# Remainders of all float32r splits on VectorE: one layer of a hybrid streaming encoder on one core

## Chip, cores and metric

The kernel runs on one core of one Trainium2 chip. The metric is the device time of one launch in microseconds, the median of several runs. The profiles are of one execution each, taken by the hardware profiler.

## The reference

One layer works on x, 1024 tokens by 1024 channels in float32, with a conditioning vector c. Both sub-layers are normed before and after, shifted, scaled and gated by rows of `c_act @ w_ada`:

```python
mod = c_act @ w_ada[l] + b_ada[l]
h = _rms(x, g_pre_mix[l]) * (1.0 + sc_m) + sh_m
p = h @ w_in[l] + b_in[l]                     # 1024 x 3072
cv = _conv_mixer(...)                         # GLU, causal depthwise conv(31), group norm, swish
hg = _hgrn2(...)                              # 4 heads, gated linear recurrence over 128 states
y = jnp.concatenate([cv, hg], axis=-1) @ w_out[l]
x = x + gt_m * _rms(y, g_post_mix[l])
h = _rms(x, g_pre_ffn[l]) * (1.0 + sc_f) + sh_f
y = jnp.square(jax.nn.relu(h @ w_up[l])) @ w_down[l]   # 4096 hidden
x = x + gt_f * _rms(y, g_post_ffn[l])
```

## The kernel before

Every large product is made from three matmuls in float32r. Each operand is split into a high part, which is the operand rounded to float32r, and a low part, the remainder: high x high, high x low and low x high are summed in PSUM. So each weight block of 128 x 1024 and each activation block is split once. ScalarE copies it into float32r (the high part), and another engine subtracts that copy from the original (the low part). This subtraction is what the change is about. Its two inputs and its output lie in SBUF.

Three places split. `split` (line 347) serves the weights of the input projection (class `Loads`, line 569), the output weights (`load_wo`, line 1140), the conv and head outputs (`conv_out`, line 774, and `put_mix`, line 639) and the summed gate rows (line 1074). `halve` (line 1312) serves channel mixing: its weights and sums come through the class `Feed` (line 1373), its activations through `hc_split` (line 1330). The first three weight blocks are split in small pieces by `first_w` (line 524), and the first activations by `h_evac` (line 504); these two have engines of their own choice, which the change leaves.

The order of the work on every engine is fixed when the program is built. The class `Weave` (line 209) keeps a planned clock for each engine. One main stream issues the large matmuls; side streams (loads, splits, evacuations, norms, heads) are Python generators that yield the time or the condition at which they go on, and `poll` runs whichever is due. The costs of the plan stand in lines 293 to 296:

```python
V = wv.engine(nc.vector, "V", lambda op, n: 0.16 + n / 930)
A = wv.engine(nc.scalar, "A", lambda op, n: 0.22 + n / 1190)
G = wv.engine(nc.gpsimd, "G", lambda op, n: 0.55 + n / (1350 if op == "tensor_scalar" else 520))
S = wv.engine(nc.sync, "S", lambda op, n: n * 1.455 / 1024)
```

On the chip each engine takes its instructions in that order, and semaphores hold them until their inputs are there and their buffers are free. `split` and `halve` choose GpSimd (G) where its planned end is at most 0.5 us (`LO_G`, line 62) behind VectorE's (V). All weight and row loads are issued on SyncE's queue (S); a load waits there until the buffer that it writes has been read by the split before.

The stages, in the order of time: the input norm and the first three blocks of the input projection; the other blocks (`ptG`, `ptU`, `ptV` by tokens, `pj` by channels), beside which the conv group (`cv`) and the four HGRN heads run; the output projection (`pout`) with the norm, gate and residual of each token tile (`out_tile`, line 1203); the second norm, transposed by TensorE (`pt` in `h2_half`, line 1230); then the up projection (`pup`) and the down projection (`al` and `be`), which use a seven-product scheme on 2 x 2 blocks, so that VectorE also forms sums of blocks.

Two chains matter below. In a head (`head_att`, line 838) seven levels follow each other, h = 1 to 64: TensorE makes a group of small matmuls `pl`, VectorE multiplies halves of Q and K in place by a decay, and the next level reads them; for the levels 1 to 8 VectorE also writes the result through a mask (four COPY_PREDICATED). Between the levels TensorE is given `pj` or `pout` matmuls. In the output projection a tile's chain is: VectorE adds the two parts of the product (`pout`), ScalarE sums squares, GpSimd makes the reciprocal root (`pr`), VectorE scales and adds the residual, ScalarE sums squares again, GpSimd makes the second root (`rx`) and scales the tile; four such tiles are needed by the first transposes `pt`.

Of the kernel before, what the change touches and what calls it, by code (L numbers as in the profile page):

```python
# [7 lines left out]
F32 = mybir.dt.float32  # L8
# [4 lines left out]
ALU = mybir.AluOpType  # L13
# [45 lines left out]


CSTEP = 8
NEAR, EXTRA, LO_G, DLAT, DLAT0 = 1.0, 0.4, 0.5, 2.0, 2.0
XIDLE, HIDLE, WIDLE = 0.3, 0.3, 0.3
XRANK, MRANK, RMODS, RCONV, RLOAD, RNORM = 0, 1, 7, 6, 3.5, 1.5
MODS_AT = 1
# [104 lines left out]
def free_size(ap):  # L170
    n = 1
    for d in ap.shape[1:]:
        n *= d
    return n
# [34 lines left out]
class Weave:  # L209
# [30 lines left out]
    def after(self, key, extra=None):  # L240
        return max(self.t[key], self.now) + (EXTRA if extra is None else extra)
# [47 lines left out]
def block_kernel(ctx: ExitStack, tc: tile.TileContext, x, vecs, masks, rows, vrow, crow, wada_t, wada_n,  # L289
                 win0, win, wint, toep, cbias, wout, wup, wdn, out):  # L290
    nc = tc.nc
    wv = Weave()
# [3 lines that stand above are left out]
# [3 lines left out]
    after, idle = wv.after, wv.idle  # L299
# [47 lines left out]
    def split(src, hi, lo):  # L347

        A.activation(hi, src, AF.Copy)
        yield after("A", 0)  # L350
        n = free_size(src)
        if max(wv.t["G"], wv.now) + 0.55 + n / 520 <= max(wv.t["V"], wv.now) + 0.16 + n / 930 + LO_G:
            G.tensor_tensor(lo, src, hi.bitcast(F32), ALU.subtract)
            yield after("G", 0)
        else:
            V.tensor_tensor(lo, src, hi.bitcast(F32), ALU.subtract)
            yield after("V", 0)


    vec = const.tile([P, V_N], F32, name="vec")  # L360
# [208 lines left out]
    class Loads:  # L569
# [6 lines left out]
        def stream(self):  # L576
            for src in self.srcs:
                yield stage.room()
                st = stage.next()
                S.dma_start(st.f, src)  # L580
                yield wv.t["S"] + DLAT
                yield self.ring.room(2)
                hi, lo = self.ring.next().r, self.ring.next().r
                yield from split(st.f, hi, lo)
                stage.give(st)
                self.ready.append((hi, lo, wv.now))
# [52 lines left out]
    def put_mix(kt, half, fn):  # L639


        if (kt // 2, half) not in mix:
            mix[kt // 2, half] = pair()
        hi, lo = mix[kt // 2, half]
        sl = HALF[kt % 2]
        full = half512("mfull")
        fn(full)
        yield from split(full, hi.r[:, sl], lo.r[:, sl])
        for n in range(4):
            marks.t["mix", kt, half * 4 + n] = wv.now  # L650
# [123 lines left out]
    def conv_out(s):  # L774

        y = ys[s]
        yield after("V")
        yield room(2)
        sz, z = new(), new()
        for h in range(2):  # L780
            yield aux_free
            pb = ps1("cpb")
            for b in range(4):
                TE.transpose(pb[:, b * P:(b + 1) * P], y.f[:, (4 * h + b) * P:(4 * h + b + 1) * P], ident)
            yield after("PE", 0.2)
            pv = pb.rearrange("p (b c i) -> p c b i", c=4, i=CB)
            zv = z.f[:, HALF[h]].rearrange("p (c b i) -> p c b i", c=4, i=CB)
            for c in range(4):
                A.activation(zv[:, c], pv[:, c], AF.Identity, bias=col(V_GNB + c), scale=col(V_GNG + c))
            done1(pb, "A")  # L790
        y.release()
        A.activation(sz.f, z.f, AF.Sigmoid)
        yield after("A")
        V.tensor_tensor(z.f, z.f, sz.f, ALU.mult)
        sz.release()
        yield after("V", 0)
        yield room(2)
        hi, lo = mix[s % 2, s // 2] = pair()
        yield from split(z.f, hi.r, lo.r)
        z.release()  # L800
        for n in 2 * s, 2 * s + 1:
            for k in range(4):
                marks.t["mix", k, n] = wv.now
# [508 lines left out]
    def halve(src, hi, lo, keep=False):  # L1312

        A.activation(hi.r, src.f, AF.Copy)
        yield after("A", 0)
        key, eng = ("G", G) if max(wv.t["G"], wv.now) + 2.5 <= max(wv.t["V"], wv.now) + 1.2 + LO_G else ("V", V)
        eng.tensor_tensor(lo.r, src.f, hi.r.bitcast(F32), ALU.subtract)
        if not keep:
            src.release()
        yield after(key, 0)  # L1320

    def plus(out, a, b, op=ALU.add):
        V.tensor_tensor(out.f, a.f, b.f, op)
# [6 lines left out]
    def hc_split(name, src, keep):  # L1330

        hi, lo = pair()
        hc.setdefault(name, []).append((hi, lo))
        yield from halve(src, hi, lo, keep)
        marks.t["hc", name, len([1 for m in marks.t if m[:2] == ("hc", name)])] = wv.now
# [73 lines left out]
    def up_single(self, names, raws, more):  # L1409
        yield from halve(raws[0], *more)  # L1410
        self.put(names[0], *more)
# [5 lines left out]
    def up_2a(self, names, raws, more):  # L1417
        g = names[0][1]
        a21, a22, a11 = raws
        yield plus(a22, a21, a22)  # L1420
        t = store(s1u, g, a22)
        yield plus(a21, a11, a21)
        wv.add(up_s3(self, names[1], a21, more[2:]), RLOAD)
        yield plus(a11, a22, a11)
        store(s2u, g, a11)
        yield from halve(a11, *more[:2], True)
        self.put(names[0], *more[:2])
        yield t
        free((a22, a11))
# [494 lines left out]
```

## Time and profile before

| | us |
|---|---|
| median of 3 runs (1122.4 to 1123.09) | 1122.75 |
| the profiled execution | 1120.97 |
| its span | 1119.2 |
| VectorE busy, 774 instructions | 705.2 |
| ScalarE busy, 651 instructions | 458.5 |
| GpSimd busy, 191 instructions | 279.8 |
| of that 65 splits of 128 x 1024 | 169.0 |
| one split of 128 x 512 on GpSimd | 1.3 |

In the views "busy" is the time in which an engine had an instruction running; the time of an instruction that is held up by another engine counts as busy too. Line numbers in the rows are mostly those of two helpers (L236 for all engines of the plan, L1808 and L1812 for TensorE, L414 for GpSimd's roots), so that groups are told apart by the names of the tiles: `s` is any of the large SBUF buffers.

### The profile page before, as it was taken

What the parts mean: (1) busy time and instruction counts of PE and PEld (TensorE: products, weight loads), DVE (VectorE), ACT (ScalarE), POOL (GpSimd) and SP (SyncE); (2) the same over time, 40 slices, a digit from 0 to 9 for tenths busy, and PEclk for the clock granted to TensorE, in tenths of its full rate; (3) what the DMA queues carried; (4) which work ended last, traced back from release to release, by engine and by line L of the source; (5) the groups of instructions that cost most, each with busy time, mean ns of one, the idle gap of its engine ahead of it and who ended that gap; (6) DMA issues with size and microseconds to landing.
All of it is one profiled execution on the core that took longest, in us unless ns stands there. A gap on an engine that the chain in (4) does not pass through costs nothing.

```text
span 1119.2 us, 18058 instructions
## 1 busy us (share of the span) xinstructions
PE 1084.5 (97%) x7524; PEld 882.9 (79%) x7524; DVE 705.2 (63%) x774; ACT 458.5 (41%) x651; POOL 279.8 (25%) x191
## 2 busy tenths in 40 slices
PE   6999999999998799989999999999999999999997
PEld 2777877878886688868888888888888888888886
DVE  3548476146789841756766965433267979996952
ACT  6732201013355243657442324466643434354530
POOL 5121013003345210672201411134400002303511
PEclk8999999999999999989999999999999999999999
DMA  9523524845212223353679744325577866675711
GB/s 366 204 75 115 160 80 135 223 138 137 75 39 96 78 75 133 125 213 133 226 257 345 287 143 171 113 70 186 196 253 273 313 219 235 217 284 176 290 50 76
DMA packets 57105, 195.27 MB, mean 174 GB/s; under 512 B 6208, under 2 KB 10688, under 8 KB 56768
## 3 DMA queue, kind: packets, MB, share of 16 engines
q1 hardware_dynamic: 57024, 194.13, 50.7%
q8 instruction: 59, 0.97, 0.4%
q14 instruction: 22, 0.18, 0.0%
HBM read 158.39 MB, written 35.72 MB: 173 GB/s over the span
## 4 chain that ended last, share of the span: by engine, by line
PE 83%; DVE 8%; POOL 3%; DMA 3%; issue 2%; ACT 1%; SPq 0%; POOLq 0%; DVEq 0%; ACTq 0%
PE pup L1808 27%; PE al L1808 15%; PE be L1808 12%; DVE s L236 8%; PE pout L1808 6%; PE pj L1808 6%; PE ptG L1808 4%; PE ptV L1808 3%; PE pf L1808 3%; POOL s L236 1%; PE po L1808 1%; PE pt L1812 1%; PE cv L1808 1%; PE pl L1808 1%; PE pm L1808 1%
## 5 line engine op out<-in xcount | busy, mean ns | idle before, releaser
L236 DVE TENSOR_TENSOR s<-s,s 128x1024 fp32r<-128x1024 f32 (+3 forms) x328 | 403.3, 1267 | 91.2 <-ACT s L236 58.2
L236 ACT ACTIVATE s<-s 128x1024 fp32r<-128x1024 f32 (+2 forms) x305 | 294.8, 997 | 343.5 <-DVE s L236 209.6
L236 POOL TENSOR_TENSOR s<-s,s 128x1024 fp32r<-128x1024 f32 (+2 forms) x81 | 187.4, 2320 | 566.3 <-ACT s L236 501.9
L1808 PE MATMUL pup<-s,s 128*128 128x512 f32 x1344 | 308.1, 390 | 0.0
L1808 PEld LDWEIGHTS pup<-s,s 128*128 128x128 f32 x1344 | 251.4, 188 | 51.9
L1808 PE MATMUL al<-s,s 128*128 128x512 f32 x768 | 175.0, 389 | 0.0
L1808 PEld LDWEIGHTS al<-s,s 128*128 128x128 f32 x768 | 144.1, 188 | 30.3 <-DVE s L236 0.4
L1808 PE MATMUL be<-s,s 128*128 128x512 f32 x576 | 131.0, 389 | 0.0
L1808 PEld LDWEIGHTS be<-s,s 128*128 128x128 f32 x576 | 108.1, 188 | 22.5
L1808 PE MATMUL pj<-s,s 128*128 128x512 f32 x432 | 107.3, 400 | 0.0
L1808 PE MATMUL pout<-s,s 128*128 128x512 f32 x384 | 95.1, 403 | 2.0 <-DVE s L236 2.0
L1808 PEld LDWEIGHTS pj<-s,s 128*128 128x128 f32 x432 | 79.8, 190 | 16.1
L1808 PEld LDWEIGHTS pout<-s,s 128*128 128x128 f32 x384 | 72.7, 193 | 17.5 <-DVE s L236 2.7
L236 DVE TENSOR_TENSOR s<-pup,s 128x1024 f32<-128x1024 f32 x24 | 29.3, 1222 | 46.7 <-PE pup L1808 46.5
L236 DVE SCALAR_TENSOR_TENSOR s<-pup,s 128x1024 f32<-128x1024 f32 x16 | 19.6, 1225 | 53.3 <-PE pup L1808 50.3
L236 DVE SCALAR_TENSOR_TENSOR s<-s,c_act,s 128x1024 f32<-128x1024 f32 x28 | 35.9, 1281 | 25.5 <-DMA s<-in_wada_n 25.4
L1808 PE MATMUL ptG<-s,s 128*128 128x512 f32 x192 | 46.2, 395 | 0.0
L1808 PE MATMUL ptU<-s,s 128*128 128x512 f32 x192 | 46.2, 395 | 0.0
L1808 PE MATMUL ptV<-s,s 128*128 128x512 f32 x192 | 46.2, 401 | 0.0
L1808 PEld LDWEIGHTS ptV<-s,s 128*128 128x128 f32 x192 | 37.0, 194 | 8.0
L236 ACT ACTIVATE junk<-s 128x1024 bf16<-128x1024 f32 (+1 forms) x30 | 30.0, 998 | 32.5 <-DVE s L236 25.3
L1808 PEld LDWEIGHTS ptG<-s,s 128*128 128x128 f32 x192 | 35.3, 188 | 7.7 <-ACT s L236 0.3
(124 smaller groups left out, 801.5 us busy)
## 6 DMA issues: line engine op xcount, KB each, us to landing
s<-in_wdn SPq DMA_DIRECT2D x72, 512.0 KB
s<-in_wup SPq DMA_DIRECT2D x56, 512.0 KB
s<-in_wada_n SPq DMA_DIRECT2D x32, 512.0 KB
s<-in_x SPq DMA_DIRECT2D x16, 512.0 KB
s<-in_wada_t SPq DMA_DIRECT2D x16, 512.0 KB
u<-s SPq DMA_DIRECT2D x16, 512.0 KB
s<-u SPq DMA_DIRECT2D x16, 512.0 KB
s<-in_wint SPq DMA_DIRECT2D x12, 512.0 KB
```

Source lines behind the costliest of these rows:

```text
L236: return op(*a, **k)
L1808: return self.te.matmul(out, lhsT=lhsT, rhs=rhs, **k)
L1812: return self.te.transpose(out, in_, identity)
```

## The change

Both choices fall away: `split` and `halve` always subtract on VectorE. The constant `LO_G` goes too.

```diff
-NEAR, EXTRA, LO_G, DLAT, DLAT0 = 1.0, 0.4, 0.5, 2.0, 2.0
+NEAR, EXTRA, DLAT, DLAT0 = 1.0, 0.4, 2.0, 2.0
...
         A.activation(hi, src, AF.Copy)
         yield after("A", 0)
-        n = free_size(src)
-        if max(wv.t["G"], wv.now) + 0.55 + n / 520 <= max(wv.t["V"], wv.now) + 0.16 + n / 930 + LO_G:
-            G.tensor_tensor(lo, src, hi.bitcast(F32), ALU.subtract)
-            yield after("G", 0)
-        else:
-            V.tensor_tensor(lo, src, hi.bitcast(F32), ALU.subtract)
-            yield after("V", 0)
+        V.tensor_tensor(lo, src, hi.bitcast(F32), ALU.subtract)
+        yield after("V", 0)
...
         A.activation(hi.r, src.f, AF.Copy)
         yield after("A", 0)
-        key, eng = ("G", G) if max(wv.t["G"], wv.now) + 2.5 <= max(wv.t["V"], wv.now) + 1.2 + LO_G else ("V", V)
-        eng.tensor_tensor(lo.r, src.f, hi.r.bitcast(F32), ALU.subtract)
+        V.tensor_tensor(lo.r, src.f, hi.r.bitcast(F32), ALU.subtract)
         if not keep:
             src.release()
-        yield after(key, 0)
+        yield after("V", 0)
```

GpSimd loses 66 instructions and VectorE has 66 more; TensorE, ScalarE and SyncE have as many as before. Since the plan's clock of VectorE runs on further, the order of the other instructions changes in places too. Three places follow.

VectorE in the stage of the last two heads, before. `s_3544`, `s_3328` and `s_3327` are Q, K and the decay of head 3, `s_3140`, `s_3039` and `s_3038` those of head 2, `s_3768` is a gate of a head.

```order
L236 COPY_PREDICATED s_682<-msk,pl 32x8x16 x4
L236 TENSOR_TENSOR s_3140<-s_3140,s_3038 128x8x64
L236 TENSOR_TENSOR s_3039<-s_3039,s_3038 128x8x64
L236 TENSOR_TENSOR s_3038<-s_3038 128x8
L236 SCALAR_TENSOR_TENSOR s_3768<-pj_3547,vec,s_3768 128x1024
L236 TENSOR_TENSOR s_3544<-s_3544,s_3327 128x256x2
L236 TENSOR_TENSOR s_3328<-s_3328,s_3327 128x256x2
L236 TENSOR_TENSOR s_3327<-s_3327 128x256
L236 COPY_PREDICATED s_682<-msk,pl 32x8x8x2 x4
L236 TENSOR_TENSOR s_3544<-s_3544,s_3327 128x128x4
```

The same place now. Head 3 has `s_3536`, `s_3322` and `s_3321`, head 2 `s_3134`, `s_3033` and `s_3032`; the gate is `s_3745`.

```order
L236 COPY_PREDICATED s_682<-msk,pl 32x8x16 x4
L236 TENSOR_TENSOR s_3743<-s_3234,s_3742 128x1024
L236 SCALAR_TENSOR_TENSOR s_3745<-pj_3539,vec,s_3745 128x1024
L236 TENSOR_TENSOR s_3134<-s_3134,s_3032 128x8x64
L236 TENSOR_TENSOR s_3033<-s_3033,s_3032 128x8x64
L236 TENSOR_TENSOR s_3032<-s_3032 128x8
L236 TENSOR_TENSOR s_3536<-s_3536,s_3321 128x256x2
L236 TENSOR_TENSOR s_3322<-s_3322,s_3321 128x256x2
L236 TENSOR_TENSOR s_3321<-s_3321 128x256
L236 COPY_PREDICATED s_682<-msk,pl 32x8x8x2 x4
L236 TENSOR_TENSOR s_3748<-s_883,s_3747 128x1024
L236 TENSOR_TENSOR s_3768<-s_3769,s_3767 128x1024
```

Three splits stand in the row that were GpSimd's: of a conv output (`s_3743`) and of two blocks of the output weights (`s_3748`, `s_3768`).

GpSimd in the norm behind the output projection, before. `s_4515` and `s_4531` are the first two token tiles, `rx` and `pr` their roots.

```order
L236 TENSOR_SCALAR s_4515<-s_4515,rx_4643 128x1024
L236 TENSOR_SCALAR pr<-pss 128x1
L414 TENSOR_TENSOR pr<-pr,mhalf 128x1
L236 TENSOR_TENSOR s_4578<-s_4575,s_4577 128x1024
L236 TENSOR_SCALAR rx_4685<-ssx2ss 128x1
L414 TENSOR_TENSOR rx_4685<-rx_4685,mhalf 128x1
L236 TENSOR_SCALAR s_4531<-s_4531,rx_4685 128x1024
```

The same place now.

```order
L236 TENSOR_SCALAR s_4515<-s_4515,rx_4643 128x1024
L236 TENSOR_SCALAR pr<-pss 128x1
L409 TENSOR_TENSOR pr<-pr,mhalf 128x1
L236 TENSOR_SCALAR rx_4685<-ssx2ss 128x1
L409 TENSOR_TENSOR rx_4685<-rx_4685,mhalf 128x1
L236 TENSOR_SCALAR s_4531<-s_4531,rx_4685 128x1024
```

The split of the first up weights (`s_4578`) is gone from between the tiles; it stands in VectorE's row now.

TensorE at the first transposes, before: three blocks of the last token tile's output projection, the transposes `pt` of the first four tiles, and that tile's fourth block. The part shown begins in the third block.

```order
L1808 MATMUL pout<-s_3925,s_3748 128x512 x2
L1808 MATMUL pout<-s_3926,s_3748 128x512 x2
L1808 MATMUL pout<-s_3925,s_3749 128x512 x2
L1812 MATMUL pt_4793<-msk,s_4515 128x128
L1812 MATMUL pt_4793<-msk,s_4531 128x128
L1812 MATMUL pt_4793<-msk,s_4573 128x128
L1812 MATMUL pt_4793<-msk,s_4550 128x128
L1808 MATMUL pout<-s_3979,s_3748 128x512 x2
```

The same place now.

```order
L1802 MATMUL pout<-s_4155,s_4292 128x512 x2
L1802 MATMUL pout<-s_4156,s_4292 128x512 x2
L1802 MATMUL pout<-s_4155,s_4293 128x512 x2
L1806 MATMUL pt_4770<-msk,s_4515 128x128
L1806 MATMUL pt_4770<-msk,s_4531 128x128
L1806 MATMUL pt_4770<-msk,s_4573 128x128
L1806 MATMUL pt_4770<-msk,s_4550 128x128
L1802 MATMUL pout<-s_3747,s_2897 128x512 x2
```

The transposes now follow on the last block of the tile before, and all eight blocks of the last tile (48 matmuls) come behind them, where there were five (30).

## The prediction

> **What bounds the kernel now.** I read the page first, for who is busy and where; then the windows of 40 us, for the stages; then TensorE's waits inside the stages that have gaps.
>
> ```profile
> span 1119.2 us, 18058 instructions
> PE 1084.5 (97%) x7524; PEld 882.9 (79%) x7524; DVE 705.2 (63%) x774; ACT 458.5 (41%) x651; POOL 279.8 (25%) x191
> ```
>
> TensorE (PE) is busy for 97% of the span, so at most 34.7 us are to be had anywhere. The windows say where (columns: busy time and count of PE, PEld, DVE = VectorE, ACT, POOL = GpSimd; granted clock, DMA share, GB/s).
>
> ```profile
> 320.00:360.00 40.00, 37.79 (x638) 29.79 (x637) 36.38 (x52) 23.02 (x41) 18.05 (x8) 1.00 0.24 81
> 360.00:400.00 40.00, 33.00 (x435) 26.94 (x434) 30.21 (x50) 15.00 (x41) 14.44 (x8) 0.96 0.27 82
> 480.00:520.00 40.00, 37.92 (x183) 30.73 (x182) 19.84 (x15) 29.55 (x40) 21.67 (x23) 0.93 0.47 168
> 600.00:640.00 40.00, 40.00 (x178) 33.12 (x177) 38.80 (x28) 11.15 (x12) 16.50 (x7) 1.00 0.83 306
> 920.00:960.00 40.00, 40.00 (x178) 33.14 (x177) 37.79 (x27) 16.00 (x16) 10.24 (x4) 1.00 0.73 248
> 960.00:1000.00 40.00, 40.00 (x179) 33.10 (x178) 38.43 (x30) 19.05 (x19) 7.59 (x3) 1.00 0.72 253
> ```
>
> In the channel-mixing stage (the last three rows) TensorE has no gap: a faster split there buys nothing, and VectorE is almost full, so there the change can only do harm. The gaps that a split can reach lie in 320 to 400 us (the last two HGRN heads beside the end of the input projection) and around 480 us (the norm behind the output projection). TensorE's waits in 330 to 410 us and in 410 to 530 us:
>
> ```profile
> PE pl L1808 <- DVE s L236: 7.6, 5, 4.3
> PE cpb L1812 <- DVE s L236: 0.7, 1, 0.7
> PE pS L1808 <- DVE s L236: 0.7, 1, 0.7
> PE pl L1808 <- ACT s L236: 0.2, 1, 0.2
> PE pt L1812 <- POOL s L236: 2.0, 1, 2.0
> PE pout L1808 <- DVE s L236: 2.0, 1, 2.0
> ```
>
> The first four rows are 9.2 us, nearly all behind VectorE. Why VectorE is late there is seen in its timeline beside GpSimd's:
>
> ```profile
> 355.22 9.02 POOL L236 TENSOR_TENSOR s<-s,s 128x1024 fp32r<-128x1024 f32 x3 [5.15 <-ACT s L236]
> 358.20 3.82 DVE L236 TENSOR_TENSOR s<-s,s 128x512 f32<-128x512 f32 x2
> 361.95 2.83 DVE L236 TENSOR_TENSOR s<-s 128x512 f32<-128x512 f32 x1
> 366.59 1.29 DVE L236 TENSOR_TENSOR s<-s,s 128x512 f32<-128x512 f32 x2
> 149.43 0.69 DVE L236 TENSOR_TENSOR s<-s 128x512 f32<-128x512 f32 x1
> ```
>
> The pair that takes 1.29 us alone takes 3.82 beside a GpSimd split, and the 0.69 us product takes 2.83: each such meeting costs VectorE 2.1 to 2.5 us. Over a long row of nothing but splits it is the same:
>
> ```profile
> 923.22 16.26 DVE L236 TENSOR_TENSOR s<-s,s 128x1024 fp32r<-128x1024 f32 x14
> 941.49 31.14 DVE L236 TENSOR_TENSOR s<-s,s 128x1024 fp32r<-128x1024 f32 x16 [2.01 <-ACT s L236]
> ```
>
> The first row runs undisturbed: 16.26/14 = 1.16 us a split. The second has six GpSimd splits beside it: (31.14 - 16 x 1.16)/6 = 2.1 us lost for each.
>
> **The change, part by part.**
>
> ```profile
> L236 POOL TENSOR_TENSOR s<-s,s 128x1024 fp32r<-128x1024 f32 x65 | 169.0, 2604 | 526.7 <-ACT s L236 501.2 <-issue 13.5 <-DMA s<-in_win 7.1
> ```
>
> *What is moved.* All 65 full splits and one half split go from GpSimd to VectorE: GpSimd loses 169.0 us and a little, VectorE gains 66 x 1.16 = 77 us of work and loses the meetings. A meeting costs 2.1 us and a moved split 1.16, so VectorE comes out ahead wherever it was busy when GpSimd split, and pays 1.16 us where it was idle. I expect its total to stay near 705 us (690 to 725).
>
> *Head stage, 320 to 400 us.* The chain is: a `pl` group on TensorE, VectorE multiplies Q and K in place (1.29 us for both), the next `pl` group; VectorE's masked copies and now the splits lie between, and TensorE's `pj` matmuls are the cover. I walked it level by level with these durations, four masked copies at 1.77 us and 18 `pj` matmuls at 4.1:
>
> ```profile
> 364.80 1.77 DVE L236 COPY_PREDICATED s<-msk,pl 32x128 f32<-32x128 uint32 x4
> 434.56 41.06 PE L1808 MATMUL pout<-s,s 128*128 128x512 f32 x180
> ```
>
> (18 x 41.06/180; the row is of `pout`, the same shape.) For head 2, a level costs VectorE 3.9 to 5.9 us with its one or two splits and TensorE 5.3 us of cover; for head 3, behind the new order, a level is 4.0 to 6.4 us against 3.2 to 7.9. At each `pl` the products of the level before are ready 1 us or more ahead. So the whole of the 9.2 us goes, and with it the slow matmuls behind its longest wait:
>
> ```profile
> 354.69 3.03 PE L1808 MATMUL pj<-s,s 128*128 128x512 f32 x12
> 366.71 1.06 PE L1808 MATMUL pl<-s,s 128*32 128x16 f32 x64 [4.31 <-DVE s L236]
> 367.70 4.03 PE L1808 MATMUL pj<-s,s 128*128 128x512 f32 x12
> 374.85 0.74 PE L1808 MATMUL pl<-s,s 128*32 128x16 f32 x64
> ```
>
> 1.06 - 0.74 + 4.03 - 3.03 = 1.3 us. Together 10.5; what is late next are splits that find their high part or their weights not there, for which I keep 1 us back. Term: -9.5 (bounds -10.5, and 0 if those waits fill the whole place).
>
> *Output projection, 450 to 500 us.* Here the end is set by a chain over VectorE, ScalarE and GpSimd that makes the normed rows which the first transposes (`pt`) need. One GpSimd split stands in the middle of it:
>
> ```profile
> 451.18 1.22 DVE L236 TENSOR_TENSOR s<-pout,s 128x1024 f32<-128x1024 f32 x1 [14.20 <-PE pout L1808]
> 462.22 2.90 POOL L236 TENSOR_SCALAR s<-s,rx 128x1024 f32<-128x1024 f32 x1
> 466.91 3.02 POOL L236 TENSOR_TENSOR s<-s,s 128x1024 fp32r<-128x1024 f32 x1
> 478.17 1.63 POOL L236 TENSOR_SCALAR s<-s,rx 128x1024 f32<-128x1024 f32 x1
> 489.18 1.12 POOL L236 TENSOR_SCALAR s<-s,rx 128x1024 f32<-128x1024 f32 x1
> 477.66 5.98 PE L1808 MATMUL pout<-s,s 128*128 128x512 f32 x18 [2.03 <-DVE s L236]
> 485.89 0.68 PE L1812 MATMUL pt<-msk,s 128*128 128x128 f32 x2 [2.04 <-POOL s L236]
> ```
>
> From the first evacuation (451.18) to the last pair of the first transposes (485.89) the chain is 34.7 us. Without the split it is 3.0 us shorter. But the new order puts the first transposes 18 matmuls earlier in TensorE's queue, ahead of the last tile, and those 18 x 41.06/180 = 4.1 us are then still to do when the chain ends: TensorE waits some 7 us in one piece where it waited 2.03 and 2.04. Counted from the first evacuation: -3.0 + 4.1 = +1.1. Bounds: -2 if VectorE, free of the 2.1 us meeting, hands on its part earlier too; +8 if GpSimd's short operations are held up more (second rival). I take +1.1.
>
> *Input stage up to 320 us, channel mixing, tail.* Up to 320 us three big splits move in 80 to 145 us and three behind 265; TensorE is not waiting there, and the cover is `ptG`, `ptU` and `pj` matmuls of 4.1 us and more between two levels: nothing (without that cover, 1.16 us for each of the six). In channel mixing, 600 to 640 us has 28 + 7 operations for VectorE, at 1.16 us 40.6 against 40 us of TensorE; 920 to 1000 has 57 + 7, 74 against 80. Behind 640 it has room again, so a backlog of under 2 us passes into the lead that the loads have: nothing, at the limit. The tail after the last matmul holds no split. Of the loads, SyncE's queue now has the output weights ahead of five blocks of W_ada, so the first gate row, whose last products stand on VectorE right ahead of the first evacuation, is late; the walk has it done some 8 us ahead of that evacuation, with each load 4 us behind the split that frees its buffer, so it costs nothing while that margin holds.
>
> For these stages a page would decide otherwise. The Trainium skill, Perfetto Trace Analysis, Optimizing Scalar/DVE Operations, says that where VectorE is saturated some of its work may well be put on another engine, GpSimd included, and adds that the two share a read port, so that between those two it might not help. By its first half the 97% of 600 to 640 us speaks against the change; by the second, and by the two rows of 1.16 and 1.95 us a split above, the work on GpSimd was no relief. The sum by the first half is the third rival below.
>
> **The sum.** -9.5 + 1.1 = -8.4 on the profiled execution's 1120.97 us, which lies 1.8 below the median of 1122.75: 1112.6 in its terms, 1114.3 in those of the median. I say 1114.
>
> **The rivals.**
>
> *Splits hold VectorE's queue.* GpSimd spent 501.2 us waiting for ScalarE's high parts at no cost; VectorE takes its work in order, and a split that waits there holds the Q and K products behind it. Eleven splits more now lie among the levels. For it: the wait of 5.15 us ahead of the row at 355.22. Against: by the walk most high parts are there 1 us or more before VectorE comes to the split. If each waits half a microsecond, 5 of the 9.5 us are lost: 1114 + 5 = 1119. Chance 0.18.
>
> *GpSimd starves.* At the output projection VectorE's row of SBUF operations is denser now, and a GpSimd operation gets through only between them: the scaling took 2.90 us beside them, 1.63 half free and 1.12 alone. If eight of the chain's short operations that ran free are each held up by 0.9 us (half of 2.90 - 1.12), the chain grows by 7 and the place is at +8: 1114 + 7 = 1121, which can't be told from no change. For it: three splits more in that row. Against: the denser row is also done sooner, and the last scalings fall behind it. Chance 0.12.
>
> *VectorE becomes the bound (slower).* If the stretch is not GpSimd's doing but VectorE's own in dense places, each moved split adds its 1.22 us to a VectorE that stays as slow. Then 600 to 640 us needs 38.80 + 7 x 1.22 = 47.3 us against 40, and 920 to 1000 needs 76.22 + 7 x 1.22 = 84.8 against 80: TensorE, without a gap there, loses 7.3 + 4.8 = 12 us, and the head stage gains nothing: 1122.75 + 12 + 1 = 1136, and from about half of that stretch staying on it is slower than before. Against it stand the undisturbed rows, for it only how full VectorE is, and an order of work that was planned anew all along. Chance 0.12, that of a smaller backlog in the same place included.
>
> **How the numbers follow.** Forecast 0.58, the three rivals 0.18, 0.12 and 0.12. A measurement tells about 0.2% (2.2 us) from no change. Faster: the forecast and the first rival, 0.76; same: the second, 0.12; slower: the third, 0.12. The range goes from 1108 (the head stage's 10.5 and the -2 of the output projection, 1110, and a little for what the faster VectorE brings elsewhere) to 1123, which takes in the first two rivals and leaves the third out.
>
> **What would show it.** Right: GpSimd's split row gone and its busy time near 110 us; undisturbed splits of 1.16 us spacing on VectorE, its busy time 690 to 725; no waits of `pl` for VectorE above 1 us in 320 to 400 and a clock of 1.00 there; one wait of `pt` for GpSimd of about 7 us; windows of 40.00 from 520 us on. Wrong: TensorE gaps behind 520 us, VectorE rows still at 2 us and more, or long VectorE waits for ScalarE among the levels.

## The result and the profile after

The changed kernel takes 1107.5 us (median of 5 runs, 1105.45 to 1110.29) against 1122.64 for the kernel before in the same session (1122.28 to 1123.09): a ratio of 0.9868 with a 95% interval of 0.9855 to 0.9881, 15 us less. The prediction said 1114 with a range from 1108: the direction is right, the gain is 1.7 times the forecast (15.1 us, where 8.7 were expected), and the median lies just below the range. The profiled execution took 1105.45 us with a span of 1103.7; it is the fastest of its five, 2 us below their median, so the places below add up to 15.5 us against the span of before.

First line, busy times and windows of the page and of the trace after (the same columns as before):

```profile
span 1103.7 us, 18008 instructions
PE 1078.7 (98%) x7524; PEld 879.6 (80%) x7524; DVE 712.6 (65%) x840; ACT 458.0 (41%) x651; POOL 106.8 (10%) x125
...
320.00:360.00 40.00, 40.00 (x647) 31.81 (x646) 37.76 (x62) 23.00 (x41) 2.58 (x2) 1.00 0.14 42
360.00:400.00 40.00, 40.00 (x427) 33.02 (x426) 28.93 (x50) 17.46 (x44) 2.95 (x2) 1.00 0.39 121
480.00:520.00 40.00, 40.00 (x199) 33.09 (x198) 24.19 (x20) 29.28 (x35) 3.74 (x6) 1.00 0.54 193
600.00:640.00 40.00, 40.00 (x178) 33.13 (x177) 33.41 (x30) 10.63 (x10) 0.00 (x0) 1.00 0.71 257
920.00:960.00 40.00, 40.00 (x179) 33.12 (x178) 36.56 (x32) 20.87 (x21) 0.00 (x0) 1.00 0.69 239
960.00:1000.00 40.00, 40.00 (x178) 33.15 (x177) 30.50 (x29) 16.85 (x17) 0.00 (x0) 1.00 0.66 237
```

GpSimd's 173 us are gone, and VectorE, with 66 more operations, is busy for only 7 us more: what it took over is paid nearly in full by what it no longer loses. In 600 to 640 us it had 38.80 us for 28 operations and has 33.41 for 30; in 920 to 1000 it had 76.22 for 57 and has 67.06 for 61. The two windows of the head stage are full, at a clock of 1.00. What is left is one wait in 400 to 530 us, at the first transposes, with GpSimd's and TensorE's rows around it:

```profile
PE pt L1806 <- POOL s L236: 4.8, 1, 4.8
```

```profile
447.75 2.92 POOL L236 TENSOR_SCALAR s<-s,rx 128x1024 f32<-128x1024 f32 x1
454.87 1.60 POOL L236 TENSOR_SCALAR s<-s,rx 128x1024 f32<-128x1024 f32 x1
461.53 1.61 POOL L236 TENSOR_SCALAR s<-s,rx 128x1024 f32<-128x1024 f32 x1
465.05 1.12 POOL L236 TENSOR_SCALAR s<-s,rx 128x1024 f32<-128x1024 f32 x1
466.22 0.69 PE L1806 MATMUL pt<-msk,s 128*128 128x128 f32 x2 [4.84 <-POOL s L236]
```

**Where the time came from.** I cut both traces at the same three points: the `pd` groups of head 0 and of head 2 on TensorE, and the first evacuation of the output projection on VectorE (451.18 before, quoted above). Before:

```profile
75.80 0.76 PE L1808 MATMUL pd<-s,s 128*32 128x32 f32 x64
318.64 0.76 PE L1808 MATMUL pd<-s,s 128*32 128x32 f32 x64
```

After:

```profile
75.89 0.76 PE L1802 MATMUL pd<-s,s 128*32 128x32 f32 x64
315.17 0.76 PE L1802 MATMUL pd<-s,s 128*32 128x32 f32 x64
436.72 1.23 DVE L236 TENSOR_TENSOR s<-pout,s 128x1024 f32<-128x1024 f32 x1 [5.74 <-PE pout L1802]
```

The input stage (first cut to second) went from 242.8 to 239.3 us, 3.5 less, where the forecast was nothing. The head stage (second to third) went from 132.5 to 121.6: 11.0 less (forecast 9.5). From the third cut to the end it was 668.0 and is 667.0: 1.0 less (forecast 1.1 more). So 5.6 of the 7.1 us of the miss came from places that the sum had at nothing or on the wrong side.

My theory on record was that the engine is the cause: GpSimd's splits stretch VectorE's operations. The rival that the result raised is that the planner's new order, which comes with the change, does a part by itself.

### The profile page after: what moved, and what is told of

The parts are those of the page before. It is cut to its first block, busy times and chain, and to the rows that moved or that the text cites. A ratio compares the mean times of both kernels' runs of the same rounds, so it can differ in the third digit from the quotient of the medians.

```text
span 1103.7 us, 18008 instructions
## 1 busy us (share of the span) xinstructions
PE 1078.7 (98%) x7524; PEld 879.6 (80%) x7524; DVE 712.6 (65%) x840; ACT 458.0 (41%) x651; POOL 106.8 (10%) x125
## 4 chain that ended last, share of the span: by engine, by line
PE 92%; POOL 2%; DVE 2%; DMA 1%; issue 1%; ACT 1%; SPq 0%; DVEq 0%; POOLq 0%; ACTq 0%
PE pup L1802 28%; PE al L1802 15%; PE be L1802 12%; PE pj L1802 8%; PE pout L1802 6%; PE ptU L1802 4%; PE ptV L1802 4%; PE ptG L1802 4%; PE pf L1802 3%; PE pl L1802 2%; DMA s<-in_x 1%; PE pt L1806 1%; PE po L1802 1%; DVE s L236 1%; PE cv L1802 1%; PE pm L1802 1%
## 5 line engine op out<-in xcount | busy, mean ns | idle before, releaser
L236 DVE TENSOR_TENSOR s<-s,s 128x1024 fp32r<-128x1024 f32 (+3 forms) x393 | 429.7, 1136 | 108.8 <-ACT s L236 77.1
```

The source lines that it names most:

```text
L236: return op(*a, **k)
```

## The experiments

**Engine and order apart: engine_only and plan_only.** The planner's order can be held while the engine is changed, and the other way round. In engine_only, the planner of before still charges GpSimd's clock for the same 66 splits, but they are issued on VectorE:

```diff
-            G.tensor_tensor(lo, src, hi.bitcast(F32), ALU.subtract)
+            nc.vector.tensor_tensor(lo, src, hi.bitcast(F32), ALU.subtract)
+            wv.spend("G", 0.55 + n / 520)
```

(and the same in `halve`). In plan_only the changed kernel's planner charges VectorE's clock, and the same 66 are issued on GpSimd (`was_g`, given the name of the calling stream, looks up the list):

```diff
-        V.tensor_tensor(lo, src, hi.bitcast(F32), ALU.subtract)
+        eng = nc.gpsimd if was_g(sys._getframe(1).f_code.co_name) else nc.vector
+        eng.tensor_tensor(lo, src, hi.bitcast(F32), ALU.subtract)
+        wv.spend("V", 0.16 + free_size(src) / 930)
```

TensorE, ScalarE and SyncE have exactly the order of before in the one and of the changed kernel in the other.

> The order of every engine's work is that of the kernel before; the 66 remainders that stood on GpSimd are issued on VectorE at the same places of the order. If the engine is the cause (meetings of a GpSimd split with VectorE's operations gone): the gains of the changed kernel in the input stage (3.5 us), the head stage (11.0) and the chain behind the output projection (3 to 5) come, and the 4.0 us that the new place of the first transposes costs are not paid: 1122.6 - 18 = 1102 to 1105 us, faster than the changed kernel by 2 to 5. If the planner's new order is the cause: no more than 5 us of the 15 come, 1118 to 1122. If VectorE's in-order queue suffers from splits that nobody planned there: slower than the changed kernel, 1108 to 1114, with waits of VectorE for ScalarE among the levels of 320 to 400 us.

> The order of every engine's work is that of the changed kernel; the same 66 remainders as before are issued on GpSimd at the places where the order has them on VectorE. If the engine is the cause: the meetings come back, and with them the waits of pl for VectorE in 320 to 400 us, on top of the 4.0 us that the transposes' new place costs: 1120 to 1128 us. If the new order is the cause: close to the changed kernel, 1106 to 1112.

Measured: engine_only 1114.98 us, ratio 0.9928 (0.991 to 0.9946); plan_only 1117.09, ratio 0.9945 (0.9927 to 0.9963). Neither theory gets its number: the engine alone brings 7 to 8 us, the order alone 5 to 6 (by the medians and by the ratios). The cuts say where (us; the changed kernel's two profiles, this one and changed_again below, agree to 0.1 in all three):

| kernel | input stage | head stage | first evacuation to end |
|---|---|---|---|
| before | 242.8 | 132.5 | 668.0 |
| engine_only | 243.6 | 126.6 | 664.3 |
| plan_only | 239.5 | 129.5 | 669.6 |
| changed | 239.3 | 121.6 | 667.0 |

The cuts come from these rows, of engine_only and of plan_only (their spans are 1111.0 and 1115.2):

```profile
76.53 0.76 PE L1810 MATMUL pd<-s,s 128*32 128x32 f32 x64
320.15 0.76 PE L1810 MATMUL pd<-s,s 128*32 128x32 f32 x64
446.73 1.23 DVE L236 TENSOR_TENSOR s<-pout,s 128x1024 f32<-128x1024 f32 x1 [14.19 <-PE pout L1810]
```

```profile
76.71 0.76 PE L1827 MATMUL pd<-s,s 128*32 128x32 f32 x64
316.19 0.76 PE L1827 MATMUL pd<-s,s 128*32 128x32 f32 x64
445.65 1.23 DVE L251 TENSOR_TENSOR s<-pout,s 128x1024 f32<-128x1024 f32 x1 [5.74 <-PE pout L1827]
```

The input stage follows the order alone, whichever engine splits. In the head stage both count: the engine takes 5.9 us, the order 3.0, both together 11.0. Behind it the engine saves 3.7 and the order costs 1.5; each kernel has one profile here, and what of these numbers is low clock is said with the output projection below.

The head stage is explained by TensorE's waits and the clock behind them. Its waits from 320 us to the first evacuation are 9.2 us before, 3.3 in engine_only, 5.9 in plan_only and none in the changed kernel; each of the first three also has about 1.7 us of low clock there (in before 5 us at 0.66, 5 x 0.34 = 1.7), the changed kernel none. With both taken off, the stage is 121.6, 121.6, 121.9 and 121.6 us. The waits for 330 to 410 us in engine_only and in plan_only:

```profile
PE pl L1810 <- DVE s L236: 2.4, 2, 1.4
PE pS L1810 <- DVE s L236: 0.7, 1, 0.7
PE tn L1814 <- DVE s L236: 0.2, 1, 0.2
```

```profile
PE pl L1827 <- DVE s L251: 4.5, 4, 2.0
PE cpb L1831 <- DVE s L251: 0.7, 1, 0.7
PE pS L1827 <- DVE s L251: 0.7, 1, 0.7
```

**The input stage: early_only and early_replanned.** Three GpSimd splits of before lie up to 180 us. early_only issues these three on VectorE in the old order (as engine_only, with the condition `wv.now < 240`). early_replanned lets the old rule choose only from 240 us of the planner's clock on, so that up to there engine and order are the changed kernel's:

```diff
-        if max(wv.t["G"], wv.now) + 0.55 + n / 520 <= max(wv.t["V"], wv.now) + 0.16 + n / 930 + LO_G:
+        if wv.now > 240 and max(wv.t["G"], wv.now) + 0.55 + n / 520 <= max(wv.t["V"], wv.now) + 0.16 + n / 930 + LO_G:
```

> The kernel before and its order, with only the three GpSimd splits of 80 to 180 us issued on VectorE. If these splits caused the waits of 0.55 us at 173 us (pl) and 0.35 us at 203 us (pm), and the second of these the clock of 0.66 in 205 to 210 us: both waits gone, a clock of 1.00 up to 240 us, and 2 to 3 us less: 1119.5 to 1120.7. If that clock is an accident of one execution: at most 0.9 us less, 1121.7 to 1122.6, and a low clock somewhere in 150 to 250 us here too. As forecast (such splits are covered): 1122.6.

> The kernel before, whose choice between the engines starts only at 240 us of the planner's clock: up to there all remainders are on VectorE and the planner knows it, so that its order up to about 240 us is that of the changed kernel; behind it the old rule. If the new order is what shortens the input stage (early_only had the engine without the order and gained nothing): the stretch from the first pd group to that of head 2 is 239.3 us instead of 242.8, with no wait of pm for VectorE near 203 us, and the heads' stage is as before: 1122.6 - 3.5 = 1119 us. If the input stage gains only with both together: the same number, which plan_only (239.5 in that stretch with the old engines) speaks against. If the 3.5 us were an accident of single executions: 1122 to 1123.

Measured: early_only 1125.15 us, ratio 1.0024 (1.001 to 1.0038), no gain, if anything slower; its input stage is 242.7. early_replanned 1115.63, ratio 0.9946 (0.9933 to 0.9958); its input stage is 239.0. The waits of the old order there, in before and in early_only:

```profile
172.98 0.70 PE L1808 MATMUL pl<-s,s 128*32 128x32 f32 x32 [0.55 <-DVE s L236]
202.78 1.95 PE L1808 MATMUL pm<-ones,s 128*128 128x1 f32 x16 [0.35 <-DVE s L236]
```

```profile
174.42 0.70 PE L1813 MATMUL pl<-s,s 128*32 128x32 f32 x32 [1.06 <-DVE s L236]
204.83 1.95 PE L1813 MATMUL pm<-ones,s 128*128 128x1 f32 x16 [0.99 <-DVE s L236]
```

Every kernel with the old order there has these two waits, 0.9 to 2.5 us in sum; no kernel with the new order has either. The new order puts 24 `ptU` matmuls instead of 18 ahead of some `pl` groups (the one at 172.98 among them), and `pm` behind 230 us. The low clock of 205 to 210 us (0.66, 1.7 us lost) is in the profile of before alone. The six other kernels with the old order have a full clock there and waits of 0.9 us (head_only) and more, and take 241.3 (chain_mid) to 243.6 us (engine_only) for the stage, 242.5 in the mean; the kernels with the new order take 239.0 to 240.2, but for transposes_late, of which more at the end. So the 3.5 us are the order's but for what that low clock added to before: by these profiles the order is worth some 3 us. The waits are the part that I can point to; which of the moved groups is worth how much was not tried.

The 6 us of early_replanned as a whole are more than this stage. Behind 240 us the old rule, starting from other clocks, spread the splits differently (the 4.31 us wait of before is 1.38 there), so its head stage is 126.3. That part says nothing about the input stage, only how much hangs on which split meets which product.

**The head stage by itself: head_only.** Before, in its own order, with the fifteen splits of 265 to 425 us on VectorE (condition `240 <= wv.now < 430`).

> The kernel before and its order, with only the fifteen GpSimd splits of the input stage's end, the heads' stage and the first output weights (about 265 to 425 us) issued on VectorE. By the term on record 9.5 us less (up to 10.5), by the trace of the changed kernel 11: 1111.6 to 1113.1, with no wait of pl for VectorE over 1 us in 320 to 400 us and a clock of 1.00 there. If the new order had a part in that gain: 1114 to 1118. If the splits hold VectorE's queue: 1116 to 1122.

Measured: 1115.79 us, ratio 0.994 (0.992 to 0.996). The second case: the stage is 126.6 us, as in engine_only, with two waits of `pl` left, 1.4 us the longest.

**The output projection: chain_one, chain_mid, transposes_late, scale_on_act.** chain_one was meant to move the one split that the prediction put in the middle of the chain; by a wrong window of the planner's clock (445 to 460) it moved the split behind it. chain_mid has the right one (435 to 445).

> The kernel before and its order, with the one GpSimd split that stands in the chain behind the output projection (at 466.91 us in the trace of before) issued on VectorE. By the term on record the chain loses 3.0 us; engine_only, where the transposes also keep their old place, lost 3.8 between the first evacuation and the first pup, but had all other splits moved too. If this one split carries the term: 41.8 to 42.6 us from the first evacuation to the first pup instead of 45.6, and 1118.5 to 1119.6 us. If it was the other splits of the stretch, or the meetings of all together: 44.5 to 45.6, 1121.5 to 1122.6.

> The kernel before and its order, with the GpSimd split at 466.91 us in the trace of before, the one in the middle of the chain, issued on VectorE. (chain_one moved the next split of that stretch, the one at 485.80 us behind the chain's end, and not this one; it changed nothing.) By the term on record, 3.0 us off the chain: the last pair of the first transposes 31.7 us behind the first evacuation instead of 34.7, from there to the end 665 to 666 us instead of 668, and 1118.5 to 1119.6 us. If GpSimd's short operations and scalings, held up by VectorE's row, set the chain with or without this split: 1121.5 to 1122.6.

Measured: chain_one 1122.33 us, ratio 1.0004 (0.9995 to 1.0013); chain_mid 1119.48, ratio 0.997 (0.9957 to 0.9983). Its last pair of first transposes stands at 483.27, 32.5 us behind the first evacuation (450.78): the one split cost 2.2 us of the 34.7 there. Where VectorE had a row of two operations in 4.56 us (at 466.45 before), it now has three in 3.5:

```profile
466.05 1.22 DVE L236 TENSOR_TENSOR s<-s,s 128x1024 f32<-128x1024 f32 x1
467.18 1.22 DVE L1322 TENSOR_TENSOR s<-s,s 128x1024 fp32r<-128x1024 f32 x1
468.32 1.22 DVE L236 TENSOR_TENSOR s<-s,s 128x1024 fp32r<-128x1024 f32 x1
```

The same pair of transposes, in engine_only and in plan_only:

```profile
479.24 0.44 PE L1814 MATMUL pt<-msk,s 128*128 128x128 f32 x2 [2.49 <-POOL s L236]
477.96 0.69 PE L1831 MATMUL pt<-msk,s 128*128 128x128 f32 x2 [7.64 <-POOL s L251]
```

Counted from the first evacuation the chain is 34.7 us before, 32.5 in engine_only, 32.3 in plan_only and 29.5 in the changed kernel (466.22). So in engine_only the chain gains what chain_mid gains, 2.2 us, with that one split; the other 1.5 of its 3.7 us is low clock that followed the pair in before (0.66 in 485 to 490 us) and did not in engine_only. The new order shortens the chain too, by 2.4 us alone; why was not tried. What it costs stands behind the pair: from there to the first matmul of the up projection (496.81 before, 481.16 in the changed kernel) it is 10.9 us before and 14.9 in the changed kernel.

transposes_late tries whether the transposes' new place costs the 4.1 us that the prediction gave it; changed_again is the changed kernel unchanged; scale_on_act takes the scaling of the normed rows off GpSimd:

```diff
         yield lambda: all(xs[half * 4 + q] for q in range(4)) and all(fcols)
+        if half == 0:
+            yield wv.now + 5.0
```

```diff
-        G.tensor_scalar(xt.f, xt.f, r, 0.0, ALU.mult, ALU.add)
         yield after("G")
+        A.activation(xt.f, xt.f, AF.Identity, scale=r)
+        yield after("A")
```

> The changed kernel, with the first transposes behind the output projection planned 5 us later, so that the last tile's matmuls stand ahead of them again, as in the kernel before. If the 4.8 us that TensorE waits there, and the low clock behind that wait, come from the transposes' place alone: most of both goes, 2.5 to 5 us less than the changed kernel, 1102.5 to 1105. If the chain over VectorE, ScalarE and GpSimd is what is late, and the transposes' place only moves the wait to the next thing that needs them (the first up projection): no change, 1106.5 to 1108.5.

> The changed kernel as it is, beside the next one on the same chip: a ratio of 0.9855 to 0.9881 to the kernel before, as measured; single executions 1105 to 1110 us, by how often the clock falls behind a wait.

> The changed kernel, with the scaling of the normed rows behind the output projection (eight operations of 128x1024 on GpSimd, 1.1 to 2.9 us each) on ScalarE. transposes_late showed that the transposes' place is not what costs there. If GpSimd's queue, without a gap from 447.75 to 468.3 us in the changed kernel, is the bound of that chain: four scalings of 2.9, 1.6, 1.6 and 1.1 us leave it, and 3 to 6 us go from the first evacuation to the end (661 to 664 us instead of 667), 1102 to 1105 us by the clock of before's 1122.6. If VectorE's dense row or ScalarE is the next bound at once: 0 to 1 us less.

Measured: transposes_late 1108.03 us, ratio 0.9868 (0.9852 to 0.9885), the changed kernel's ratio to the last digit; in its profile it is 1.1 us shorter from the first evacuation to the end (665.9), with a wait of 2.18 us of `pout` for VectorE where the 4.84 stood. changed_again 1106.41, ratio 0.9861 (0.9841 to 0.9881). scale_on_act 1103.17, ratio 0.9826 (0.9809 to 0.9843): 3.2 us below changed_again on the same chip, the fastest kernel of the study; from its first evacuation (438.43) to its end (1101.7) it is 663.3 us instead of 667.0. GpSimd's queue has hardly a gap from 447.75 to 468.3 us in the changed kernel. Its fourth normed row is ready 29.45 us behind the first evacuation (the scaling at 465.05, quoted above), in transposes_late as well, and in scale_on_act after 27.3 us. So the scalings on GpSimd cost that chain 2.2 us, wherever the transposes stand. Whether they cost it by their time in GpSimd's queue or by what they took from VectorE beside them was not told apart. A scaling that took 1.12 to 2.92 us on GpSimd takes 1.13 to 1.16 on ScalarE, here the fourth, and TensorE is busy nearly throughout at a full clock, where the changed kernel has it busy for 5.2 us of 10. In scale_on_act TensorE waits 2.1 us for ScalarE later on, in 475 to 480 us. Windows of TensorE in the changed kernel, one scaling and windows of all engines in scale_on_act:

```profile
460.00:465.00 5.00, 1.39 (x8) 0.85 0.88 296
465.00:470.00 5.00, 3.78 (x13) 0.50 0.30 120
```

```profile
464.56 1.16 ACT L236 ACTIVATE s<-s,rx 128x1024 f32<-128x1024 f32 x1 [0.18 <-POOL rx L409]
```

```profile
460.00:465.00 5.00, 4.83 (x21) 3.66 (x20) 5.00 (x5) 4.58 (x7) 3.14 (x6) 1.00 0.93 291
465.00:470.00 5.00, 5.00 (x25) 4.14 (x24) 4.88 (x5) 4.07 (x7) 1.56 (x3) 1.00 0.71 276
```

This kernel also has its transposes planned later (the planner counts ScalarE's scaling behind GpSimd's root), as in transposes_late, so its gain is that of the scaling with that place, against 1.1 us of the place alone in one profile and none in the median.

**The channel mixing: mixing_only.** Before, in its own order, with the 45 splits from 480 us of the planner's clock on VectorE, two thirds of all that the change moves.

> The kernel before and its order, with the 45 GpSimd splits of the channel mixing issued on VectorE: two thirds of all that the change moves. As forecast (TensorE has no gap there to lose): within 0.2% of before, 1120.4 to 1124.8, and VectorE's busy time in 920 to 1000 us below the 76.2 us of before or near it. If the engine's gain is spread over the program: 3 to 5 us less. If VectorE becomes the bound around 600 to 640 us: 2 to 12 us more, with TensorE below 40.00 there.

Measured: 1121.15 us, ratio 0.9992 (0.9982 to 1.0003): nothing. VectorE has 70.7 us in 920 to 1000 for 65 operations, against 76.2 for 57 before, and TensorE is at 40.00 in all windows shown:

```profile
600.00:640.00 40.00, 40.00 (x179) 33.10 (x178) 37.73 (x34) 12.21 (x13) 0.00 (x0) 1.00 0.85 309
920.00:960.00 40.00, 40.00 (x178) 33.14 (x177) 36.59 (x33) 18.87 (x20) 0.00 (x0) 1.00 0.64 230
960.00:1000.00 40.00, 40.00 (x178) 33.10 (x178) 34.11 (x32) 17.87 (x18) 0.00 (x0) 1.00 0.70 258
```

**The disputed cost by itself: meeting.**

> A kernel of its own that leaves the layer out and writes part of x: rows of 16 VectorE operations of 128x1024, alone and beside 6 GpSimd operations of the same shape, one pair of forms after another. By the meeting of the prediction (2.1 us lost by VectorE for each GpSimd subtraction): 16 x 1.16 = 18.6 us alone and 18.6 + 6 x 2.1 = 31 us beside six subtractions. If the stretch comes from both engines reading SBUF: about 18.6 us for the VectorE form whose first operand lies in PSUM, beside the same GpSimd subtractions. If it comes from anything that GpSimd does: 31 there too. If VectorE's stretch were its own (third rival of the prediction): 18.6 us in every row. Beside ScalarE copies: 18.6.

This kernel leaves the layer out and has only such rows; it ran once. Each pair of rows is one stretch, GpSimd's six operations (`w`) and VectorE's sixteen (`v`) started together; `a` and `b` lie in SBUF, `ps` in PSUM:

```profile
27.97 14.42 POOL L52 TENSOR_TENSOR wb<-c,d 128x1024 fp32r<-128x1024 f32 x6
42.88 18.81 POOL L52 TENSOR_TENSOR wc<-c,d 128x1024 fp32r<-128x1024 f32 x6
45.16 30.20 DVE L40 TENSOR_TENSOR vc<-a,b 128x1024 fp32r<-128x1024 f32 x16
75.93 10.99 POOL L55 TENSOR_SCALAR wd<-c 128x1024 fp32r<-128x1024 f32 x6
76.90 23.67 DVE L40 TENSOR_TENSOR vd<-a,b 128x1024 fp32r<-128x1024 f32 x16
101.13 14.49 POOL L52 TENSOR_TENSOR we<-c,d 128x1024 fp32r<-128x1024 f32 x6
103.41 20.09 DVE L46 TENSOR_TENSOR ve<-ps,b 128x1024 fp32r<-128x1024 f32 x16
182.67 20.10 DVE L40 TENSOR_TENSOR vh<-a,b 128x1024 fp32r<-128x1024 f32 x16
```

With nothing of GpSimd beside it (`vh`, beside ten ScalarE copies) VectorE's row takes 20.10 us, 1.26 us an operation, where the kernel's own undisturbed row had 1.16. Beside six GpSimd subtractions it takes 30.20 (`vc`): 10.1 us more, and since the first of the six began 2.3 us ahead of VectorE's row and was nearly done, that is 10.1/5 = 2.0 us a meeting (1.7 over all six), against the 2.1 of the prediction. GpSimd pays too, 18.81 against 14.42 alone. Beside six GpSimd scalings, which read one operand, VectorE loses 3.6 us (`vd`). With its first operand in PSUM it loses nothing, and neither does GpSimd (`ve`). One operand is not always enough to be clear of it: sixteen VectorE scalings of one SBUF operand took 22.36 us beside six GpSimd subtractions, which took 16.20 instead of 14.42; a quiet row of such scalings was not run. The rows with two SBUF operands and with one in PSUM agree with the Trainium skill, SBUF — State Buffer, Who interferes with whom: a VectorE instruction with two SBUF inputs contends with a GpSimd instruction that reads SBUF, and one with at most one SBUF input, outside the faster modes, does not.

## Why the prediction was right or wrong

*Head stage, -9.5: right, measured -11.0.* All of the 9.2 us of waits went, and 1.7 of low clock; the 1 us that I kept back for late high parts was not needed. But the reason I gave, the meetings, carries only 5.9 us: with the old order 3.3 us of waits stay (engine_only, head_only). My walk was over the new order's levels, so the number held, while the words gave the engine what order and engine do together.

*Input stage, "TensorE is not waiting there ... nothing": this step failed, measured -3.5.* It was waiting there: 0.55 and 0.35 us behind VectorE stood in the trace of before, and I read the waits only from 330 us on. The runs showed that it is the order that removes them (plan_only and early_replanned have the gain, engine_only and early_only do not). I had taken the moved order as a thing to cost at one place, the transposes, and not as a term of its own at every place where a `pl` group or a `pm` got more cover.

*Output projection, -3.0 + 4.1 = +1.1: measured -1.0.* The chain term was mis-sized: the chain lost 5.2 us, not 3.0. The split that I named carries 2.2 of it (chain_mid, engine_only), and the new order, to which I gave nothing there, 2.4 alone (plan_only). The 4.1 for the matmuls left behind the chain held, at 4.0. As a price of the transposes' place it is too much, since transposes_late, without it, gains 1.1 us in its profile and nothing in the median. The wait is 4.84 us where I said some 7; the terms themselves give 2.03 + 2.04 - 3.0 + 4.1 = 5.2. What I did not name is that GpSimd's scalings are a part of that chain's bound (scale_on_act).

*Channel mixing and tail, nothing: right* (mixing_only; 622.4 us from the first up projection to the end before, 622.5 after).

*The rivals.* That splits hold VectorE's queue did not happen in the changed kernel: no `pl` wait in the head stage. GpSimd's starving is there in part (2.92 us for a scaling that takes 1.12 free), at the size that it had before. VectorE as the bound fell altogether: its row in 600 to 640 us became shorter by 5.4 us with two more operations in it. Of the two halves of what the Trainium skill, Perfetto Trace Analysis, Optimizing Scalar/DVE Operations, says, the second held (between these two engines offloading might not help), as the meeting's rows show.

*The sum.* The terms miss by 3.5, 2.1 and 1.5 us, 7.1 of the 15.5. The range ended at 1108 because I gave the order no gain outside the head stage. Nor were the 34.7 us in which TensorE had no work all that was to be had: its busy time fell too, by 5.8 us (1084.5 to 1078.7), in part because less of it ran at a low clock.

*What stays open:* which moved group is worth what in the input stage, why the new order shortens the chain behind the output projection, and how far the order's gain is a planner that now counts VectorE's real load or only a luckier draw. early_replanned, whose later splits fell differently by another start alone, shows that such draws are worth several us here.

## What to carry to other kernels

Count an operation on GpSimd with what it takes from VectorE: here a subtraction of 2.4 us on GpSimd cost VectorE 1.7 to 2.0 us, more than the 1.16 to 1.26 us of doing it there, where both of VectorE's own operands lay in SBUF. When a change also moves a planner's order, make the order a term at every place where the critical engine waits, however short the wait; a run with the old order on the new engine, and one the other way round, tells the two apart. And when one link of a chain is taken out, look for the engine of the chain that has no gap left: here that was where the next gain lay.

## What the runs showed of the hardware

The granted clock falls for a fixed time. In windows of 1 us of the kernel before it is at about 0.50 from 206.0 to 209.5 us, which the windows of 5 us show as one 0.66: 3.4 us at half the clock, 1.7 us lost. The other falls behind 75 us and ahead of the last microseconds of these traces are of the same size, twice or three times that: 0.95 and 0.71 in engine_only (375 to 385 us, 1.7 us), 0.85, 0.50 and 0.97 in the changed kernel (460 to 475 us, 3.4 us, in part of which TensorE was idle anyway).

It falls behind waits that look alike in some executions and not in others. In the kernel before it fell to 0.66 for 5 us behind a wait of 0.35 us at 202.78; in chain_mid and in engine_only it stayed at 1.00 behind 0.37 and 1.43 us at the same group. In transposes_late a wait of 2.01 us was followed by this (windows of TensorE; the clock is the number behind the count):

```profile
230.00:235.00 5.00, 3.42 (x169) 1.00 0.56 208
235.00:240.00 5.00, 4.58 (x85) 0.55 0.01 3
240.00:245.00 5.00, 5.00 (x12) 0.50 0.34 105
```

With 0.92 in the next 5 us that is 5.1 us lost, three times 1.7, and its input stage took 245.0 us instead of 239.3 in the same order. Of the changed kernel's executions the fastest had a mean clock of 0.995 and the slowest (1110.29 us) one of 0.990. The Trainium skill, TensorE: Matmul & The Clock Gate, HAM oscillation — how this bites in real kernels, gives as a rule that TensorE should have no idle gap over about 3.4 us. In these runs a low clock also followed gaps of 0.35 and 2.0 us, so a gap under that length did not ensure a full clock. That these waits caused the falls is not shown: in the kernel before, 3.2 us lie between the end of the wait and the fall, and the 16 matmuls of one column (`pm`) take the first 1.95 of them.
